# Seven-product gate groups: the fifth sum borrows an accumulator tile, and one of the four summed weight blocks is made by an adding transfer from DRAM

## The chip, the cores and the metric

The kernel runs on one core of one Trainium2 chip. The metric is the device time of that core in microseconds (us), the median of several runs. The core has a matrix engine (TensorE, "PE" in the profile), a vector engine ("DVE"), a scalar engine ("ACT"), a general engine ("POOL") and a queue engine ("SP") that here only issues transfers. Each engine works through its own instructions strictly in program order; what one engine needs of another it waits for with semaphores.

## The reference

Two layers, each on 256 tokens of width 2048. One wide input projection feeds three token mixers and, per mixer b, a sigmoid gate of width 2048:

```python
h = rms_norm(x, norm_w)
proj = h @ w_in
(qa, ka, va, za, qi, ki, wi, ub, zb, qc, kc, vc, zc, gates) = jnp.split(proj, split_points(), axis=-1)
...
y_a = (dsa_attention(...) * jax.nn.silu(za)) @ w_a_out
y_b = (conformer_conv(...) * jax.nn.silu(zb)) @ w_b_out
y_c = (stick_breaking_attention(...) * jax.nn.silu(zc)) @ w_c_out
g = jax.nn.sigmoid(gates).reshape(b, s, N_BRANCH, D_MODEL)
merged = g[:, :, 0] * y_a + g[:, :, 1] * y_b + g[:, :, 2] * y_c
return x + merged @ w_out
```

What matters here are the gates, `h @ w_in[:, gate columns]`, and the products that run between them: the last of `za` and `zb`, and `y_b`, `y_c`, `y_a`.

## The kernel before

**A plain product.** Weights stay in DRAM in float32. A unit is two blocks of 128 rows by 512 columns (512 KB): SP loads it into one of six `raw` tiles, ACT rounds it to the matrix engine's float32r format (`wh`, line 279), and DVE takes what the rounding lost (`wl`, line 284); three tiles of each exist. The activations have been split the same way, so one unit makes three passes (high by high, low by high, high by low) for each of two token blocks: 12 matmuls of 512 columns, all at line 295. `chunk_steps` sums a 512-column chunk over 16 units (or 8, for the branch products) in an accumulator tile `acc` of two PSUM banks; two such tiles exist, in turn, so that one can be read out while the next is filled. After each unit `chunk_steps` yields.

**A seven-product group.** Three of the twelve 512-column pairs of gate chunks in a layer (the list `FAST`) are made by Strassen's scheme in Winograd's form, in the generator `strassen`: two token blocks by two column blocks, the input dimension halved, so that seven block products stand for eight. One product of one unit is 6 matmuls. Each of the four units u of a half is worked off in turn. In the first loop, per u: o1 with block b11, o5 with s5 = b11 + b12, o6 with s6 = s5 + b22, o7 with s7 = b12 + b22. The sums are DVE instructions (`summands`, line 1195). The partial results live in two `mm` tiles of two banks each, one bank per sum. Then the outputs c11, c21 and c22 are formed (lines 1238 to 1242), and the second loop adds, per u: o1 with b21, o7 with s4 = s6 + b21 (again a DVE sum at line 1195, into the place of s6, kept since the first loop), and o5 with b22, which is loaded a second time.

**How both are woven together.** `combine` runs the plain work of this stage: second half of `za`, then `zb` (two chunks), a gate chunk, the four chunks of `y_b`, a gate chunk, the four chunks of `y_c`, the four of `y_a`. After each of its units, a budget `owed` grows by `RATES[kind]`; as long as it is not negative, `advance_fast` takes one step of the group, and the step's own yield (1, 2 or 3) is taken off. A scheduler then puts each engine's instructions in order, those marked high priority first; casts (`high`), differences (`low`), sums and the read-outs of accumulators are so marked. Read-outs differ: `za` and `zb` are read by ACT as two 16-bit copies (`turn_in`, line 172), gate chunks by two Tanh on ACT (line 962), and branch chunks by one DVE instruction that also applies the gate (lines 1157 and 1159).

**The POOL queue.** Gates and parked activations are fetched and stored through `paced`: ACT copies three columns of the newest `wh` (line 245), POOL copies those (line 246), and POOL then issues the transfer, so that it starts no earlier than that point of the weight stream.

Of the kernel before, what the change touches and what calls it, by code (L numbers as in the profile page):

```python
# [15 lines left out]
P = 128  # L16
# [15 lines left out]
TAKEN = -3e38  # L32
RATES = (1.85, 1.85, 1.8, 1.9)
TURN = (8, 8)
# [19 lines left out]
def trunk(ctx: ExitStack, tc: tile.TileContext, x, xt, w_in, w_a, w_b, w_c, w_out,  # L54
# [6 lines left out]
    dp = ctx.enter_context(tc.tile_pool(name="scratch", bufs=1, space=bass.MemoryType.DRAM))  # L61
    ap = ctx.enter_context(tc.tile_pool(name="acc", bufs=2, space=bass.MemoryType.PSUM))
    mp = ctx.enter_context(tc.tile_pool(name="mm", bufs=2, space=bass.MemoryType.PSUM))
# [58 lines left out]
    def mm_tile():  # L122
        return mp.tile([P, 1024], F32, tag="mm", name=nm("mm"))

    def acc_tile():
        return ap.tile([P, 2, 512], F32, tag="acc", name=nm("acc"))

# [113 lines left out]

    def paced(dst, src):
        mark, copy = small(3, 12), small(5, 4)
        with tc.high_priority():
            nc.scalar.copy(mark, landed[0][:, 0, 0:3])  # L245
        seen = nc.gpsimd.tensor_copy(copy[:, :3], mark)  # L246
        with tc.issue_after(seen.ins):
            nc.gpsimd.dma_start(dst, src)

# [106 lines left out]
    def chunk_steps(w, segs, act, nk, ku=2, whole=False):  # L356
        acc = acc_tile()
        n = sum(c for _, c in segs)
        accs = [acc[:, t, :] for t in range(NT)]
        for k0 in range(0, nk, ku):  # L360
            background(token_products(accs, n, unit(w, k0, ku, segs), act, k0, ku, nk, range(NT)))
            yield
        return acc if whole else accs
# [158 lines left out]
    for layer in range(DEPTH):  # L522
# [681 lines left out]
        def strassen(b, jj):  # L1204
            c0 = O_G + b * D + jj * 1024
            kept = []
            pa, pb = mm_tile(), mm_tile()
            o1, o5, o6, o7 = pa[:, :512], pa[:, 512:], pb[:, :512], pb[:, 512:]
            def block(k0, c, u):
# [8 lines left out]
            for u in range(4):  # L1218
# [6 lines left out]
                summands(s5, b22, dst=s6)  # L1225
                kept.append(s6)
                yield 2
                product(o6, mixed(1), u, halves(s6))
                s7 = summands(b12, b22)
                yield 2  # L1230
                product(o7, mixed(3), u, halves(s7))
                if u < 3:
# [4 lines left out]
            with tc.high_priority():  # L1237
                nc.scalar.copy(c11, o1)
                nc.vector.tensor_add(c21, o6, c11)
                nc.vector.tensor_add(c22, o7, c21)  # L1240
                nc.vector.tensor_sub(c22, o5, c22)
                nc.scalar.activation(c22, c22, AF.Tanh, scale=0.5)
            yield 3
            for u in range(4):
                b21 = block(KC, 0, u)
                product(o1, plain(0, KC), u, halves(b21), True)
                s4 = summands(kept[u], b21, dst=kept[u])
                yield 1
                product(o7, plain(1, KC), u, halves(s4), True)
                yield 2  # L1250
                product(o5, mixed(2), u, halves(block(KC, 512, u)), True)
                yield 1
            with tc.high_priority():
                nc.scalar.activation(c11, o1, AF.Tanh, scale=0.5)
                nc.vector.tensor_sub(c12, o5, c21)
                nc.vector.tensor_add(c21, o7, c21)
                nc.scalar.activation(c12, c12, AF.Tanh, scale=0.5)
                nc.scalar.activation(c21, c21, AF.Tanh, scale=0.5)
# [18 lines left out]
        owed = 0  # L1277
        for _ in combine():
            owed += RATES[kind[0]]
            for _ in range(2):  # L1280
                if back:
                    back.pop(0)()
            while owed >= 0 and fast_:
                owed -= advance_fast()

# [126 lines left out]
```

## Time and profile before

Median 2006.66 us of 3 runs (2006.46 to 2009.44). The profiled execution took 2007.48 us, and its span, from the first to the last instruction, is 2005.6 us.

| | busy, us | share of the span | instructions |
|---|---|---|---|
| PE (matmuls) | 1993.7 | 99% | 9518 |
| DVE | 1614.1 | 80% | 1758 |
| ACT | 1402.9 | 70% | 1988 |
| POOL | 119.5 | 6% | 176 |
| read from / written to HBM | 419.59 MB / 23.07 MB | | |
| profiled execution | 2007.48 us | span 2005.6 us | mean granted clock 0.998 |

Both layers pass through the same stages; the woven stage lies at about 560 to 895 us in the first layer and 1555 to 1890 us in the second. Its mean DMA rate is 282 and 285 GB/s there. A row of grouped instructions reads: line, engine, operation, output and input, count, then busy us and mean ns of one. A window row gives busy us and the number of instructions (x) of PE, PE's weight load, DVE, ACT and POOL in that stretch, then the granted clock, the DMA share and GB/s.

### The profile page before, as it was taken

How to read it: one execution, taken by the hardware profiler on the slowest of the kernel's cores; microseconds unless marked ns; L12 is line 12 of the kernel's file. 1: busy time of each engine (PE TensorE's matmuls, PEld its weight loads, DVE VectorE, ACT ScalarE, POOL GpSimd, SP SyncE). 2: the span in 40 equal slices, each digit the busy share in tenths (PEclk: the TensorE clock that was granted, in tenths of full speed). 3: DMA queues.
4: the chain of work that ended last, by engine and by line, in shares of the span. 5: the costliest groups of instructions: out<-in, count | busy, mean ns of one | idle time of the engine just before them, and what ended most of it. 6: DMA issues, size and time to landing. Idle time of an engine off the chain costs nothing.

```text
span 2005.6 us, 26820 instructions
## 1 busy us (share of the span) xinstructions
PE 1993.7 (99%) x9518; PEld 1686.6 (84%) x9518; DVE 1614.1 (80%) x1758; ACT 1402.9 (70%) x1988; POOL 119.5 (6%) x176
## 2 busy tenths in 40 slices
PE   9999999999999999999999999999999999999998
PEld 7888889988888888878888888899888888888887
DVE  8687787897998887886676887778979988878865
ACT  7699877667786755566666997776677776555653
POOL 0000000000000203300000000000000002133000
PEclk9999999999999999999999999999999999999999
DMA  8788667768789879998967776576688999799973
GB/s 281 211 228 214 170 177 211 220 179 219 211 260 288 267 255 302 301 288 250 264 199 213 217 214 177 159 223 207 189 212 219 281 276 281 250 305 316 289 247 126
DMA packets 350902, 471.17 MB, mean 235 GB/s; under 512 B 109488, under 2 KB 167600, under 8 KB 350640
## 3 DMA queue, kind: packets, MB, share of 16 engines
q1 hardware_dynamic: 329216, 425.01, 72.3%
q0 software_dynamic: 20096, 41.95, 7.1%
q10 hardware_dynamic: 1456, 2.51, 0.4%
q8 instruction: 74, 1.21, 0.2%
q14 instruction: 60, 0.49, 0.1%
HBM read 419.59 MB, written 23.07 MB: 221 GB/s over the span
## 4 chain that ended last, share of the span: by engine, by line
PE 96%; DMA 1%; DVE 1%; ACT 1%; issue 0%; ACTq 0%; SPq 0%; DVEq 0%
PE acc L295 82%; PE mm L295 11%; DMA raw<-in_w_in_dram 1%; DVE wl L284 1%; PE mm L940 1%; PE mm L970 1%; ACT wh L279 0%; PE mm L1010 0%; PE mm L805 0%; PE mm L761 0%; PE mm L914 0%; PE mm L789 0%; PE mm L807 0%; DMA cst<-in_consts_dram 0%; PE mm L764 0%
## 5 line engine op out<-in xcount | busy, mean ns | idle before, releaser
L295 PE MATMUL acc<-wh,s 128*128 128x512 f32 (+2 forms) x4480 | 1092.3, 386 | 1.5 <-ACT wh L279 1.5
L284 DVE TENSOR_TENSOR wl<-raw,wh 128x1024 fp32r<-128x1024 f32 (+2 forms) x706 | 848.2, 1208 | 280.0 <-ACT wh L279 258.8
L279 ACT CAST wh<-raw 128x1024 fp32r<-128x1024 f32 (+2 forms) x705 | 730.4, 1040 | 389.1 <-PE acc L295 263.5
L295 PEld LDWEIGHTS acc<-wh,s 128*128 128x128 f32 x4480 | 828.2, 188 | 167.8 <-ACT wh L279 2.4
L295 PE MATMUL acc<-wl,s 128*128 128x512 f32 (+2 forms) x2240 | 589.4, 385 | 0.0
L295 PEld LDWEIGHTS acc<-wl,s 128*128 128x128 f32 x2240 | 415.4, 188 | 84.2 <-DVE wl L284 0.4
L474 ACT ACTIVATE t<-s,cst 128x255 f32<-128x255 f32 (+14 forms) x480 | 201.1, 487 | 0.1
L295 PE MATMUL mm<-wh,s 128*128 128x512 f32 x672 | 180.2, 390 | 0.4 <-ACT wh L279 0.2
L295 PEld LDWEIGHTS mm<-wh,s 128*128 128x128 f32 x672 | 125.7, 188 | 28.0 <-ACT wh L279 1.7
L477 DVE TENSOR_TENSOR s<-s,t 128x1020 f32<-128x1020 f32 (+14 forms) x120 | 138.7, 1156 | 3.4 <-ACT t L474 2.7
L295 PE MATMUL acc<-s,wh 128*128 128x384 f32 (+1 forms) x608 | 126.4, 348 | 0.0
L295 PEld LDWEIGHTS acc<-s,wh 128*128 128x128 f32 x608 | 104.2, 189 | 3.1
L295 PE MATMUL mm<-wl,s 128*128 128x512 f32 x336 | 104.1, 391 | 0.2
L279 ACT CAST wh<-s 128x1024 fp32r<-128x1024 f32 x48 | 50.4, 1049 | 54.6 <-DVE s L1195 31.7
L295 PEld LDWEIGHTS acc<-s,wl 128*128 128x128 f32 x608 | 79.2, 191 | 1.0
L295 PE MATMUL acc<-s,wl 128*128 128x192 f32 (+1 forms) x608 | 79.7, 273 | 0.0
L284 DVE TENSOR_TENSOR wl<-s,wh 128x1024 fp32r<-128x1024 f32 x48 | 58.8, 1225 | 22.0 <-ACT wh L279 21.7
L295 PEld LDWEIGHTS mm<-wl,s 128*128 128x128 f32 x336 | 62.7, 188 | 15.0 <-DVE wl L284 2.3
L963 POOL DMA_DIRECT2D gates<-t x12 | 8.9, 739 | 1113.1 <-ACT t L962 1112.5
L279 ACT CAST wh<-t 128x1024 fp32r<-128x1024 f32 x48 | 50.4, 1050 | 32.4 <-PE acc L295 19.0
L246 POOL COPY sm<-sm 128x3 f32<-128x3 f32 x68 | 53.8, 801 | 310.9 <-ACT sm L245 310.9
L284 DVE TENSOR_TENSOR wl<-t,wh 128x1024 fp32r<-128x1024 f32 x48 | 58.7, 1224 | 13.9 <-ACT wh L279 10.4
(248 smaller groups left out, 1294.7 us busy)
## 6 DMA issues: line engine op xcount, KB each, us to landing
raw<-in_w_in_dram SPq DMA_DIRECT2D x578, 512.0 KB, 4.5
raw<-in_w_out_dram SPq DMA_DIRECT2D x64, 512.0 KB, 5.0
raw<-in_w_b_dram SPq DMA_DIRECT2D x32, 512.0 KB, 5.8
raw<-in_w_c_dram SPq DMA_DIRECT2D x32, 512.0 KB, 5.9
raw<-in_w_a_dram SPq DMA_DIRECT2D x32, 512.0 KB, 6.3
t<-gates POOLq DMA_DIRECT2D x20, 512.0 KB, 7.2
s<-parked POOLq DMA_DIRECT2D x32, 256.0 KB, 7.4
gates<-t POOLq DMA_DIRECT2D x12, 512.0 KB, 6.6
```

Of the source, the lines that this page charges most:

```text
L246: seen = nc.gpsimd.tensor_copy(copy[:, :3], mark)
L279: highs[0] = nc.scalar.copy(u[1], u[0])
L284: sub = nc.vector.tensor_sub(u[2], u[0], u[1].bitcast(F32))
L295: newest[0] = nc.tensor.matmul(o, lhsT, rhs, start=start, stop=stop, skip_group_check=True)
L474: nc.scalar.activation(o[:, i, :S - d], yT[:, c, :S - d], AF.Copy, scale=wq)
L477: sums.append(lambda: nc.vector.tensor_add(to, to, o[:, :, :S - d]))
L940: nc.tensor.matmul(ps[:, q * S:(q + 1) * S], qb2[i][:, g * 4 + q, :], ki[:, j, 0, :], start=n == 0, stop=n == 2)
L963: nc.gpsimd.dma_start(gates[b][:, :, j * 512:(j + 1) * 512].rearrange("t p d -> p t d"), sg_)
L970: nc.tensor.matmul(ps[:, q * n:(q + 1) * n], qaT[:, c * 4 + q, ts_], kaT[:, c, :n], start=True, stop=True)
```

## The change

Five sums now run in the first loop: the product o3 with b22 moves there, so that b22 is used while it is still in its `raw` tile, and the second loop has two products instead of three. The fifth sum needs a PSUM bank, and both `mm` tiles are full; `lend` takes the accumulator tile that the running chunk does not use. The two accumulator tiles get names of their own (`acc`, `acd`), and while one is lent, every chunk uses the other one. The loan ends after the first loop, when o3 has been read. At the end of a chunk inside the loan (`chunk_steps` now yields True there) at least two steps of the group are put between it and the next. The sum s4 is made by an adding transfer: b21 is sent from DRAM by POOL onto s6 (`paced(..., accum_op=ALU.add)`), once o6's operands have been made from s6. `RATES` goes down, since a group has fewer steps of larger yield. The four outputs are formed with the same five DVE instructions in another order. The number of matmuls does not change.

```diff
-RATES = (1.85, 1.85, 1.8, 1.9)
+RATES = (1.7, 1.7, 1.7, 1.75)
...
+    turn_of = [0]
+    lent = [None]
     def acc_tile():
-        return ap.tile([P, 2, 512], F32, tag="acc", name=nm("acc"))
+        turn_of[0] = 1 - turn_of[0] if lent[0] is None else 1 - lent[0]
+        return ap.tile([P, 2, 512], F32, tag=("acc", "acd")[turn_of[0]], name=nm("acc"))
+
+    def lend():
+        lent[0] = 1 - turn_of[0]
+        return ap.tile([P, 2, 512], F32, tag=("acc", "acd")[lent[0]], name=nm("acc"))[:, 0, :]
...
-            yield
+            yield k0 + ku == nk
...
-            o1, o5, o6, o7 = pa[:, :512], pa[:, 512:], pb[:, :512], pb[:, 512:]
+            o1, o7, o5, o6 = pa[:, :512], pa[:, 512:], pb[:, :512], pb[:, 512:]
+            o3 = lend()
...
                 summands(s5, b22, dst=s6)
-                kept.append(s6)
                 yield 2
                 product(o6, mixed(1), u, halves(s6))
                 s7 = summands(b12, b22)
                 yield 2
+                product(o3, mixed(2), u, halves(b22))
+                kept.append(s6)
+                paced(s6, place(KC, 0, u), accum_op=ALU.add)
+                yield 1
                 product(o7, mixed(3), u, halves(s7))
...
-                nc.vector.tensor_add(c22, o7, c21)
-                nc.vector.tensor_sub(c22, o5, c22)
+                nc.vector.tensor_sub(c12, o5, c21)
+                nc.vector.tensor_sub(c22, c12, o7)
+                nc.vector.tensor_add(c12, o3, c12)
...
+            lent[0] = None
...
             for u in range(4):
-                b21 = block(KC, 0, u)
-                product(o1, plain(0, KC), u, halves(b21), True)
-                s4 = summands(kept[u], b21, dst=kept[u])
+                product(o1, plain(0, KC), u, halves(block(KC, 0, u)), True)
                 yield 1
-                product(o7, plain(1, KC), u, halves(s4), True)
-                yield 2
-                product(o5, mixed(2), u, halves(block(KC, 512, u)), True)
+                product(o7, plain(1, KC), u, halves(kept[u]), True)
                 yield 1
...
-        for _ in combine():
+        for ends in combine():
...
-            while owed >= 0 and fast_:
-                owed -= advance_fast()
+            if True:
+                least = 2 if ends and lent[0] is not None else 0
+                while (owed >= 0 or least > 0) and fast_:
+                    least -= 1
+                    owed -= advance_fast()
```

Three places show how the order moves. They are told for the first layer; the second has the same order. In changed rows the line numbers are shifted: 295 became 303, 279 became 287, 284 became 292, 172 became 180, 188 became 196.

**PE, where zb's first chunk ends.** Before, the chunk's accumulator is `acc_5417` and the next chunk's is `acc_5674`, in the other tile:

```order
L295 MATMUL mm_5162<-wl_5643,s_775_4565 128x512 x2
L295 MATMUL acc_5417<-wh_5653,s_11_102 128x512 x8
L295 MATMUL acc_5417<-wl_5654,s_11_102 128x512 x4
L295 MATMUL acc_5674<-wh_5676,s_8_99 128x512 x8
L295 MATMUL acc_5674<-wl_5677,s_8_99 128x512 x4
```

Now the chunk's accumulator is `acc_5432`, the next one's `acc_5710` in the same tile, and `acc_5163` is o3 in the lent tile:

```order
L303 MATMUL acc_5432<-wh_5663,s_11_102 128x512 x8
L303 MATMUL acc_5432<-wl_5664,s_11_102 128x512 x4
L303 MATMUL mm_5162<-wh_5680,s_772_4562 128x512 x4
L303 MATMUL mm_5162<-wl_5681,s_772_4562 128x512 x2
L303 MATMUL mm_5162<-wh_5694,s_773_4563 128x512 x4
L303 MATMUL mm_5162<-wl_5695,s_773_4563 128x512 x2
L303 MATMUL acc_5163<-wh_5751,s_774_4564 128x512 x4
L303 MATMUL acc_5710<-wh_5712,s_8_99 128x512 x8
```

Where the next chunk followed at once, 16 matmuls of the group now stand between.

**ACT, at the same place.** Before, the two copies that read `acc_5417` out:

```order
L279 CAST wh_5653<-raw_5652 128x1024
L279 CAST wh_5676<-raw_5675 128x1024
L279 CAST wh_5701<-raw_5700 128x1024
L188 COPY t_940_5413<-t_941_5414 128x1024
L279 CAST wh_5723<-raw_5721 128x1024
L172 COPY t_992_5670<-acc_5417 128x2x512
L1238 COPY t_998_5693<-mm_5161 128x512
L172 COPY t_992_5670<-acc_5417 128x2x512
```

And now those that read `acc_5432` (`raw_5690` is b22, and `wh_5751` is o3's operand):

```order
L287 CAST wh_5680<-t_987_5632 128x1024
L287 CAST wh_5694<-s_999_5692 128x1024
L287 CAST wh_5712<-raw_5711 128x1024
L196 COPY t_944_5428<-t_945_5429 128x1024
L287 CAST wh_5733<-raw_5732 128x1024
L180 COPY t_1003_5706<-acc_5432 128x2x512
L287 CAST wh_5751<-raw_5690 128x1024
L180 COPY t_1003_5706<-acc_5432 128x2x512
```

The cast for o3, whose matmuls stand ahead of the next chunk on PE, stands on ACT behind the casts of the next chunk's first two units, behind a copy of an older chunk and behind the first read-out copy; the second read-out copy is last.

**DVE, in the second loop of the third group, during y_a.** Before (`s_1346_7251` is a kept s6, which becomes s4):

```order
L284 TENSOR_TENSOR wl_7763<-raw_7760,wh_7762 128x1024
L1195 TENSOR_TENSOR s_1346_7251<-s_1346_7251,raw_7760 128x1024
L284 TENSOR_TENSOR wl_7774<-s_1346_7251,wh_7773 128x1024
L1159 SCALAR_TENSOR_TENSOR t_1441_7646<-t_1441_7646,acc_7652 128x1024
L284 TENSOR_TENSOR wl_7799<-raw_7797,wh_7798 128x1024
```

Now (`s_1361_7285` is a kept s6 onto which the transfer has added b21):

```order
L1171 TENSOR_TENSOR s_878_5135<-s_878_5135,t_1464_7708 128x1024
L292 TENSOR_TENSOR wl_7862<-raw_7860,wh_7861 128x1024
L292 TENSOR_TENSOR wl_7883<-raw_7880,wh_7882 128x1024
L292 TENSOR_TENSOR wl_7894<-raw_7892,wh_7893 128x1024
L292 TENSOR_TENSOR wl_7911<-s_1361_7285,wh_7910 128x1024
L292 TENSOR_TENSOR wl_7923<-raw_7920,wh_7922 128x1024
```

The sum between the two differences of one u is gone.

More of the change, by code (lines that the diff above doesn't have):

```diff
@@ L61, in trunk @@
     dp = ctx.enter_context(tc.tile_pool(name="scratch", bufs=1, space=bass.MemoryType.DRAM))
-    ap = ctx.enter_context(tc.tile_pool(name="acc", bufs=2, space=bass.MemoryType.PSUM))
+    ap = ctx.enter_context(tc.tile_pool(name="acc", bufs=1, space=bass.MemoryType.PSUM))
     mp = ctx.enter_context(tc.tile_pool(name="mm", bufs=2, space=bass.MemoryType.PSUM))
@@ L240, in trunk, with paced @@
     highs = [None]
-    def paced(dst, src):
+    def paced(dst, src, **kw):
         mark, copy = small(3, 12), small(5, 4)
@@ L247, in paced @@
         with tc.issue_after(seen.ins):
-            nc.gpsimd.dma_start(dst, src)
+            nc.gpsimd.dma_start(dst, src, **kw)
     def operands(shape):
@@ L1207, in strassen, with place @@
             pa, pb = mm_tile(), mm_tile()
-            o1, o5, o6, o7 = pa[:, :512], pa[:, 512:], pb[:, :512], pb[:, 512:]
+            o1, o7, o5, o6 = pa[:, :512], pa[:, 512:], pb[:, :512], pb[:, 512:]
+            o3 = lend()
+            def place(k0, c, u):
+                return w[(k0 + 2 * u) * P:(k0 + 2 * u + 2) * P, c0 + c:c0 + c + 512].rearrange("(k p) c -> p k c", p=P)
             def block(k0, c, u):
@@ L1239, in strassen @@
                 nc.vector.tensor_add(c21, o6, c11)
-                nc.vector.tensor_add(c22, o7, c21)
-                nc.vector.tensor_sub(c22, o5, c22)
+                nc.vector.tensor_sub(c12, o5, c21)
+                nc.vector.tensor_sub(c22, c12, o7)
+                nc.vector.tensor_add(c12, o3, c12)
                 nc.scalar.activation(c22, c22, AF.Tanh, scale=0.5)
+                nc.scalar.activation(c12, c12, AF.Tanh, scale=0.5)
+            lent[0] = None
             yield 3
             for u in range(4):
-                b21 = block(KC, 0, u)
-                product(o1, plain(0, KC), u, halves(b21), True)
-                s4 = summands(kept[u], b21, dst=kept[u])
+                product(o1, plain(0, KC), u, halves(block(KC, 0, u)), True)
                 yield 1
-                product(o7, plain(1, KC), u, halves(s4), True)
-                yield 2
-                product(o5, mixed(2), u, halves(block(KC, 512, u)), True)
+                product(o7, plain(1, KC), u, halves(kept[u]), True)
                 yield 1
@@ L1254, in strassen @@
                 nc.scalar.activation(c11, o1, AF.Tanh, scale=0.5)
-                nc.vector.tensor_sub(c12, o5, c21)
                 nc.vector.tensor_add(c21, o7, c21)
-                nc.scalar.activation(c12, c12, AF.Tanh, scale=0.5)
                 nc.scalar.activation(c21, c21, AF.Tanh, scale=0.5)
```

## Prediction

> **What bounds the kernel now.** I read the page's first part, then who PE waited for, then windows of 50 us, to see whether PE has anything to give.
>
> ```profile
> span 2005.6 us, 26820 instructions
> PE 1993.7 (99%) x9518; PEld 1686.6 (84%) x9518; DVE 1614.1 (80%) x1758; ACT 1402.9 (70%) x1988; POOL 119.5 (6%) x176
> ...
> PE 96%; DMA 1%; DVE 1%; ACT 1%; issue 0%; ACTq 0%; SPq 0%; DVEq 0%
> ```
> ```profile
> PE acc L295 <- ACT wh L279: 1.5, 2, 1.1
> PE mm L657 <- DVE eps L75: 1.1, 1, 1.1
> PE mm L562 <- DVE t L682: 0.3, 1, 0.3
> PE mm L295 <- ACT wh L279: 0.2, 1, 0.2
> ```
>
> PE is the chain (96%), and its visible waits are about 3 us in 2005.6. The number of matmuls stays, so time can only come from moments in which PE runs thinner than it could. Since ends of matmuls are modelled, I count starts instead of waits:
>
> ```profile
> 800.00:850.00 50.00, 50.00 (x222) 41.42 (x221) 43.03 (x38) 27.91 (x37) 16.14 (x25) 1.00 0.99 302
> 850.00:900.00 50.00, 49.59 (x214) 39.35 (x213) 41.93 (x39) 31.61 (x34) 2.41 (x4) 1.00 0.95 291
> ...
> 1800.00:1850.00 50.00, 50.00 (x222) 41.40 (x221) 43.85 (x39) 27.70 (x37) 15.57 (x26) 1.00 1.00 305
> 1850.00:1900.00 50.00, 49.82 (x218) 40.30 (x217) 42.05 (x39) 32.94 (x35) 1.55 (x3) 1.00 0.96 295
> ```
>
> A full window holds 222 starts, 50 / 222 = 0.225 us each. The windows that end the woven stage hold 214 and 218: 8 and 4 are missing, 1.8 and 0.9 us. **All that the woven stages lose is 2.7 us**, at a granted clock of 1.00; every other window between 560 and 850 us holds 222 or 223. What ends last in the gaps stands in the chain:
>
> ```profile
> 849.93 14.59 DMA raw<-in_w_in_dram
> ...
> 866.85 1.23 DVE s L1195
> ...
> 868.17 1.06 ACT wh L279
> ...
> 869.26 1.24 DVE wl L284
> ...
> 870.54 0.73 PE mm L295 x2
> ```
>
> From 866.85 on it is the second loop's sum s4: sum, cast, difference, then matmul, 3.7 us in series (around 880 and in the second layer at 1871 it is the same).
>
> **The change part by part.** My base is the profiled execution, 2007.48 us (span 2005.6 and 1.9 around it); the median shown, 2006.66, lies 0.82 lower, and I carry the sum over to it.
>
> *s4 goes from DVE.* Two layers with three groups of four units make 24 sums:
>
> ```profile
> L1195 DVE TENSOR_TENSOR s<-s,raw 128x1024 f32<-128x1024 f32 x24 | 29.3, 1219 | 0.0
> ```
>
> 29.3 us of DVE work go, but DVE is not the bound; only the serial path in the gaps is worth something. Without s4, the second loop's two products per unit need 2 differences of 1.22 us for 12 matmuls (2.7 us), and the cast of a kept block can start as soon as a `wh` tile is free. What is late next there is the landing of b21. I take the full **-2.7 us**; its ends are 0 (DMA was the cause after all) and -2.7.
>
> *The loads.* 24 second loads of b22 disappear from SP, but b21 now crosses twice, once as operand and once in the adding transfer: 24 x 512 KB move from the SP queue to POOL's, and HBM read stays at 419.59 MB. So nothing is gained where DMA binds. What an adding transfer from DRAM costs is not in the trace; the nearest rows are the one from SBUF and a plain fetch on the same queue:
>
> ```profile
> raw<-in_w_in_dram SPq DMA_DIRECT2D x578, 512.0 KB, 4.5
> ...
> t<-gates POOLq DMA_DIRECT2D x20, 512.0 KB, 7.2
> ...
> s<-t POOLq DMA_DIRECT2D x8, 512.0 KB, 7.8
> ```
>
> The result is needed only in the second loop, tens of us later, so its 7.8 us are hidden; adding may cost the shared DMA engines 7.8 - 7.2 = 0.6 us. If each one held the weight stream up by that, 24 x 0.6 = 14.4 us; but PE feels late loads only where it already ran thin, in the third group, so 8 x 0.6 = **4.8 us is my upper end**. The lower end is 0, since fewer SP loads cannot give PE more than the 2.7 us above. I take **0**, by the row nearest to a price on PE:
>
> ```profile
> ACT wh L279 <- DMA raw<-in_w_in_dram: 26.4, 14, 3.7
> ```
>
> ACT already waits 26.4 us for weights, and PE loses at most those 2.7.
>
> *Marks.* Each adding transfer brings a mark on ACT and a copy on POOL:
>
> ```profile
> L246 POOL COPY sm<-sm 128x3 f32<-128x3 f32 x68 | 53.8, 801 | 310.9 <-ACT sm L245 310.9
> ...
> L245 ACT COPY sm<-wh 128x3 f32<-128x3 f32 x68 | 10.1, 191 | 2.5
> ```
>
> 24 x 0.19 = 4.6 us on an ACT that is 70% busy, and 24 x 0.8 on an idle POOL. Behind them in POOL's queue stand only gate and parked transfers, needed a chunk later: nothing.
>
> *One accumulator for the chunks.* This is a new wait: a chunk's first matmul waits until the chunk before it has been read out, and everything behind it on PE waits too. Until now a whole chunk hid that. The cover now is the group steps between, and I go through the boundaries with these rows:
>
> ```profile
> L284 DVE TENSOR_TENSOR wl<-raw,wh 128x1024 fp32r<-128x1024 f32 x686 | 834.0, 1222 | 262.0 <-ACT wh L279 245.1 <-ACT t L771 10.0 <-ACT t L1242 3.8
> ...
> L1159 DVE SCALAR_TENSOR_TENSOR t<-t,acc 128x1024 f32<-128x1024 f32 x16 | 19.5, 1218 | 4.8 <-PE acc L295 4.7
> ```
> ```profile
> L962 ACT ACTIVATE t<-acc 128x512 f32<-128x512 f32 x24 | 13.4, 591 | 0.0
> ```
> ```profile
> 589.11 1.04 ACT L279 CAST wh<-raw 128x1024 fp32r<-128x1024 f32 x1
> 590.06 1.00 ACT L172 COPY t<-acc 128x1024 uint16<-128x1024 uint16 x1
> 590.96 1.05 ACT L279 CAST wh<-t 128x1024 fp32r<-128x1024 f32 x1
> 591.91 1.01 ACT L172 COPY t<-acc 128x1024 uint16<-128x1024 uint16 x1
> 593.15 1.06 ACT L279 CAST wh<-raw 128x1024 fp32r<-128x1024 f32 x1 [0.24 <-PE acc L295]
> ...
> 621.77 1.36 ACT L188 COPY t<-t 128x1024 uint16<-128x1024 uint16 x1
> 623.08 1.06 ACT L279 CAST wh<-raw 128x1024 fp32r<-128x1024 f32 x1
> ```
> ```profile
> 591.14 1.98 PE L295 MATMUL acc<-wh,s 128*128 128x512 f32 x8
> 592.96 1.07 PE L295 MATMUL acc<-wl,s 128*128 128x512 f32 x4
> 593.86 1.07 PE L295 MATMUL mm<-wh,s 128*128 128x512 f32 x4
> 594.77 0.62 PE L295 MATMUL mm<-wl,s 128*128 128x512 f32 x2
> 595.22 1.07 PE L295 MATMUL mm<-wh,s 128*128 128x512 f32 x4
> ```
>
> A unit of a chunk takes 593.86 - 591.14 = 2.72 us, a group product 1.36. Back to back, a cast on ACT takes 0.95 us and a read-out copy 0.90, an older copy (L188) 623.08 - 621.77 = 1.31; the cast at 593.15 begins 0.19 us after 592.96, where PE left the `wh` tile that it fills (three tiles, reused in turn). Let T be the moment when PE passes a chunk's last matmul.
>
> The seven boundaries per layer that DVE reads out, behind y_b's and y_c's chunks: two products cover 2.72 us; in the order, the read-out stands behind the differences for just those two products and at most one sum. By the reuse of the `wl` tiles these are done by about T + 0.5, so it ends by T + 0.5 + 1.22 = T + 1.7: 1.0 us to spare, no wait. The two behind gate chunks are read by two Tanh of 0.59 us from T + 0.24, done by T + 1.4; the covers are 2.72 and 1.36: nothing. za's end: first copy at T + 0.24, a cast, second copy from T + 2.1, done at T + 3.1; the cover is 14 matmuls, 3.17: just nothing.
>
> zb's first end is the one that doesn't fit. ACT's order there: the cast of the next chunk's first unit, once its tile is free at T - 0.91 + 0.19 = T - 0.72; the older copy from T + 0.23; the second cast T + 1.54; the first read-out copy T + 2.49; the cast for o3 T + 3.39, done at T + 4.4. PE has 12 matmuls until then and wants o3 at T + 2.72: **it waits 1.7 us**, and with the 0.1 us that PE loses on restarting (the pair at 870.54, after a stall, takes 0.73 where 0.62 is normal, as at 594.77) 1.8. Then 4 matmuls, until T + 5.35, meet the second copy's end at T + 5.3. Both layers have this order: 2 x 1.8 = **+3.7 us**, unrounded. The ends: 0, if ACT runs further ahead, and 2 x (2.7 + 1.8), if the older copy also waits for its transposes.
>
> Sum: -2.7 + 0 + 3.7 = +1.0. From 2007.48 that is 2008.5; carried to the median, **2007.7 us**.
>
> **A rule against the change.** The boundary rows above say that reading out hides behind the group's products. The Trainium skill, Perfetto Trace Analysis, section Matmuls, advises rotating independent matmul groups through different PSUM banks so that the reading-out of one overlaps the next group's matmuls. By that rule every boundary now shows a wait. The trace agrees that rotation works (no PE wait at any boundary before), but has no run without it; the second rival below prices that.
>
> **The rivals.**
> 1. *No boundary waits.* ACT has slack, and PE's order might find o3's cast early. Against it: casts can't pass the copies in ACT's order. Then 2006.66 - 2.7 = 2004.0, within 0.2%.
> 2. *The cover is too short at DVE's boundaries: slower.* Today DVE reads out late, without harm:
>
> ```profile
> 852.38 1.98 PE L295 MATMUL acc<-wh,s 128*128 128x512 f32 x8
> ...
> 854.34 1.21 DVE L1159 SCALAR_TENSOR_TENSOR t<-t,acc 128x1024 f32<-128x1024 f32 x1
> ```
> The read-out started 1.96 us after its chunk was passed at 852.38. With 1.22 for itself it would end at 3.18, 0.46 beyond a cover of 2.72. It decides from a start later than T + 1.5. For it: that row. Against: three output sums stood ahead there, and at the new boundaries none does. 14 x 0.46 = 6.4 on top of my sum: 2014.1.
> 3. *The gaps at the end stay*, since loads and not s4 make them: the load at 849.93 took 14.59 us in the chain, where 4.5 is the median. Then 2007.7 + 2.7 = 2010.4, still within 0.2%.
> 4. *Adding transfers crowd the weight stream* in the third group, where the DMA share is already 0.99 and 1.00: 2007.7 + 4.8 = 2012.5, slower.
> 5. *Faster by over 0.2%* (4.0 us) would need more than the 2.7 us that PE loses: no row offers it.
>
> **How the numbers follow.** About 0.2% is what a measurement of this kernel can tell from no change: 2002.6 to 2010.7. Chances: forecast 0.45, rival 1 0.20, rival 3 0.12, rival 2 0.10, rival 4 0.08, rival 5 0.05. Same: 0.45 + 0.20 + 0.12 = 0.77; slower 0.18; faster 0.05. The range runs from rival 1 to rival 4, 2003.8 to 2012.5, and leaves out rivals 2 and 5.
>
> **What would show it.** Right: windows that end the woven stage hold 222 again; no instruction at line 1203 (once 1195) that writes a kept `s`; near 625 and 1620 us a PE wait of about 1.7 us on ACT, for o3's `wh`; SP's queue down to about 412 MB, POOL's up to 54. Wrong: PE waits on DVE's read-out at chunk ends, new waits on DMA in the third group, or gaps left at 850 to 900.

## The result, and the profile after

The changed kernel takes **2024.11 us** (median of 4 runs, 2023.72 to 2025.23), the kernel before beside it 2008.05 us (4 runs, 2006.46 to 2009.94): a ratio of 1.0081, 95% interval 1.0063 to 1.0098. It is slower by 16 us, and outside the predicted range. Its profiled execution took 2023.76 us with a span of 2022.0.

The prediction's own list of signs comes first. These are the queues and the memory traffic on the page of after (packets, MB, share):

```profile
q1 hardware_dynamic: 322688, 412.43, 70.4%
q0 software_dynamic: 26624, 54.53, 10.2%
HBM read 419.59 MB, written 23.07 MB: 219 GB/s over the span
```

SP's queue is down to 412 MB and POOL's up to 54, with the same read: the transfers moved as foretold. Next, what PE waited for in after (us in total, times, longest):

```profile
PE mm L303 <- DVE t L1257: 8.3, 2, 4.2
PE acc L303 <- ACT wh L287: 4.2, 3, 1.9
```

Two of the three waits in the second row, 1.95 and 1.94 us, are the foretold wait on ACT. The first was not foretold: twice, PE waits for the vector sum at line 1257, one of the four that form a group's outputs. The windows of PE alone (busy us, starts of matmuls, granted clock, DMA share, GB/s) say what each place costs:

```profile
600.00:650.00 50.00, 48.05 (x205) 0.97 1.02 269
...
850.00:900.00 50.00, 45.77 (x195) 0.97 0.96 286
1600.00:1650.00 50.00, 48.06 (x213) 1.00 1.04 291
...
1850.00:1900.00 50.00, 45.97 (x191) 0.93 0.97 291
```

With those from 740 to 790 and from 1740 to 1790 us, which are full (222 each), these windows start 1248 matmuls; before they started 1320 (first row of the table below). The 72 that are missing, at 0.225 us each, are 16.2 us, and the span grew by 16.4: nearly the whole loss lies in four places (a further wait of 0.8 us, near 1510 us, lies outside the woven stage). The end of zb's first chunk (near 625 and 1629 us) lost 17 + 9 = 26 starts, 5.9 us. The third group's turn from its first to its second loop (near 871 and 1873 us) lost 19 + 27 = 46 against before, 10.4 us, although the 8 + 4 that were missing there before should have come back. Against a full window it lost 27 + 31 = 58, 13 us.

The timeline of after at that turn (start us, us, engine, line, operation, what ended the idle time before):

```profile
868.26 0.58 ACT L1254 COPY t<-mm 128x512 f32<-128x512 f32 x1
...
869.54 0.68 DVE L1255 TENSOR_TENSOR t<-mm,t 128x512 f32<-128x512 f32 x1
...
870.26 0.69 DVE L1256 TENSOR_TENSOR t<-mm,t 128x512 f32<-128x512 f32 x1
870.31 1.07 PE L303 MATMUL acc<-wl,s 128*128 128x512 f32 x4
872.56 1.05 ACT L287 CAST wh<-raw 128x1024 fp32r<-128x1024 f32 x1 [3.71 <-DMA raw<-in_w_in_dram]
...
873.63 1.23 DVE L292 TENSOR_TENSOR wl<-raw,wh 128x1024 fp32r<-128x1024 f32 x1 [2.69 <-ACT wh L287]
874.78 0.68 DVE L1257 TENSOR_TENSOR t<-t,mm 128x512 f32<-128x512 f32 x1
...
875.60 0.94 PE L303 MATMUL mm<-wh,s 128*128 128x512 f32 x3 [4.23 <-DVE t L1257]
```

Read it from below. PE's next product goes into o1, whose tile now also holds o7, and L1257 is the sum that reads o7. L1257 could have run at 870.95, behind L1256, but DVE's order has the difference of b21 between them, and that waits for the cast of a block that landed late (ACT idle 3.71 us on a DMA). The order of the two kernels at this place, before (its lines 1240 and 1241 are the sums, `wl_7692` is b21's difference) and after (`wl_7841`):

```
L1240 TENSOR_TENSOR t_1440_7638<-mm_7050,t_1439_7637 128x512
L1241 TENSOR_TENSOR t_1440_7638<-mm_7049,t_1440_7638 128x512
L1159 SCALAR_TENSOR_TENSOR t_1398_7482<-t_1398_7482,acc_7488 128x1024
L284 TENSOR_TENSOR wl_7692<-raw_7689,wh_7691 128x1024
```
```
L1255 TENSOR_TENSOR t_1479_7779<-mm_7078,t_1479_7779 128x512
L1256 TENSOR_TENSOR t_1480_7780<-mm_7078,t_1479_7779 128x512
L292 TENSOR_TENSOR wl_7841<-raw_7838,wh_7840 128x1024
L1257 TENSOR_TENSOR t_1480_7780<-t_1480_7780,mm_7077 128x512
L1258 TENSOR_TENSOR t_1480_7780<-acc_7079,t_1480_7780 128x512
```

Before, every sum stood ahead of the block's difference; now two stand behind it. There are also more of them: of the five DVE instructions that form a group's outputs, three stood at the turn before and four do now, so it is not quite "the same five DVE instructions in another order".

The loads were not this late before either. The kernel before, DMA issues from 840 to 880 us (count, KB each, median us from issue to landing):

```profile
raw<-in_w_a_dram SPq DMA_DIRECT2D x9, 512.0 KB, 7.5
raw<-in_w_in_dram SPq DMA_DIRECT2D x7, 512.0 KB, 9.3
```

In after the medians of these two rows are 12.3 and 14.3 us. The turn also lies elsewhere: its last sum began at 853.73 us before and at 875.49 after.

### The profile page after: what moved, and what is told of

It is laid out like the page before. It is cut to its first block, busy times and chain, and to the rows that moved or that the text cites. A ratio compares the mean times of both kernels' runs of the same rounds, so it can differ in the third digit from the quotient of the medians.

```text
span 2022.0 us, 26932 instructions
## 1 busy us (share of the span) xinstructions
PE 1998.7 (99%) x9518; PEld 1691.1 (84%) x9518; DVE 1589.7 (79%) x1734; ACT 1406.2 (70%) x2012; POOL 165.0 (8%) x224
## 4 chain that ended last, share of the span: by engine, by line
PE 64%; issue 31%; DMA 2%; ACT 1%; DVE 1%; POOL 0%; ACTq 0%; SPq 0%; DVEq 0%; POOLq 0%
PE acc L303 53%; PE mm L303 9%; DMA raw<-in_w_in_dram 1%; ACT wh L287 1%; DMA t<-t 0%; DVE wl L292 0%; DMA raw<-in_w_c_dram 0%; PE mm L1018 0%; DMA gates<-t 0%; PE mm L948 0%; PE mm L978 0%; ACT t L999 0%; DMA cst<-in_consts_dram 0%; PE mm L813 0%; PE mm L769 0%
## 5 line engine op out<-in xcount | busy, mean ns | idle before, releaser
L303 PE MATMUL acc<-wh,s 128*128 128x512 f32 (+2 forms) x4576 | 1122.9, 387 | 4.2 <-ACT wh L287 4.2
L303 PEld LDWEIGHTS acc<-wh,s 128*128 128x128 f32 x4576 | 849.0, 189 | 176.8 <-ACT wh L287 5.4
L303 PE MATMUL acc<-wl,s 128*128 128x512 f32 (+2 forms) x2288 | 604.1, 385 | 0.8 <-DVE wl L292 0.8
L303 PEld LDWEIGHTS acc<-wl,s 128*128 128x128 f32 x2288 | 425.3, 188 | 87.1 <-DVE wl L292 1.3
L303 PE MATMUL mm<-wh,s 128*128 128x512 f32 x576 | 155.5, 391 | 8.3 <-DVE t L1257 8.3
L303 PEld LDWEIGHTS mm<-wh,s 128*128 128x128 f32 x576 | 108.3, 188 | 31.5 <-issue 9.0
L254 POOL COPY sm<-sm 128x3 f32<-128x3 f32 x92 | 75.0, 819 | 358.6 <-ACT sm L253 358.5
L303 PE MATMUL mm<-wl,s 128*128 128x512 f32 x288 | 88.6, 389 | 0.0
L303 PEld LDWEIGHTS mm<-wl,s 128*128 128x128 f32 x288 | 54.1, 188 | 11.2
```

The source lines that it names most:

```text
L303: newest[0] = nc.tensor.matmul(o, lhsT, rhs, start=start, stop=stop, skip_group_check=True)
```

## The experiments

Every run is the changed kernel with one edit, or with edits joined. The table has the starts of matmuls in the same six windows of each profiled run, so that a place can be compared (222 is full; one execution each, and a place shifts by some us between runs), the median and the ratio to the kernel before.

| run | 600 to 650 | 740 to 790 | 850 to 900 | 1600 to 1650 | 1740 to 1790 | 1850 to 1900 | span, us | median, us | ratio, 95% interval |
|---|---|---|---|---|---|---|---|---|---|
| before | 222 | 222 | 214 | 222 | 222 | 218 | 2005.6 | 2008.05 | |
| after | 205 | 222 | 195 | 213 | 222 | 191 | 2022.0 | 2024.11 | 1.0081, 1.0063 to 1.0098 |
| e1 pairing | 204 | 222 | 193 | 203 | 223 | 193 | 2023.9 | 2025.58 | 1.0088, 1.0071 to 1.0105 |
| e3 sum on DVE | 212 | 201 | 190 | 213 | 200 | 189 | 2031.5 | 2034.35 | 1.0137, 1.0120 to 1.0154 |
| e4 more cover | 221 | 193 | 188 | 219 | 192 | 190 | 2039.2 | 2041.36 | 1.0168, 1.0153 to 1.0183 |
| e5 earlier | 216 | 192 | 223 | 219 | 193 | 223 | 2020.5 | 2023.38 | 1.0077, 1.0062 to 1.0092 |
| e6 sums ahead | 205 | 222 | 204 | 205 | 222 | 216 | 2015.9 | 2013.97 | 1.0028, 1.0017 to 1.0040 |
| e7 load early | 206 | 222 | 181 | 205 | 222 | 186 | 2027.6 | 2028.51 | 1.0099, 1.0084 to 1.0114 |
| e8 cover za, zb | 221 | 222 | 197 | 221 | 222 | 189 | 2020.9 | 2022.71 | 1.0074, 1.0059 to 1.0089 |
| e9: e6 + e7 + e8 | 221 | 222 | 185 | 221 | 222 | 187 | 2024.8 | 2026.33 | 1.0093, 1.0078 to 1.0108 |
| e10: e6 without adding | 212 | 223 | 210 | 212 | 221 | 218 | 2011.7 | 2015.21 | 1.0036, 1.0024 to 1.0048 |
| e11: e6 + e8 | 222 | 223 | 215 | 221 | 221 | 216 | 2012.2 | 2013.10 | 1.0027, 1.0016 to 1.0038 |
| e12: e6 + e5 | 216 | 199 | 222 | 220 | 195 | 222 | 2017.2 | 2018.89 | 1.0058, 1.0041 to 1.0075 |
| e13: e6 + burst sooner | 212 | 223 | 214 | 213 | 222 | 221 | 2010.2 | 2012.82 | 1.0027, 1.0016 to 1.0037 |
| e14: e6 + copy on DVE | 218 | 222 | 217 | 218 | 222 | 214 | 2013.6 | 2015.39 | 1.0036, 1.0022 to 1.0049 |
| e15: e6 + e13 + e14 | 218 | 222 | 212 | 217 | 222 | 221 | 2010.1 | 2013.79 | 1.0031, 1.0019 to 1.0043 |

### e1: the tiles paired as before

```diff
-            o1, o7, o5, o6 = pa[:, :512], pa[:, 512:], pb[:, :512], pb[:, 512:]
+            o1, o5, o6, o7 = pa[:, :512], pa[:, 512:], pb[:, :512], pb[:, 512:]
```

> Only the assignment of the four sums to the two tiles goes back to that of the kernel before (o1 and o5 in one tile, o6 and o7 in the other). Theory T (shared tile): at the start of the third group's second loop PE's first product writes o1 in a tile that also holds o7, and waits for the vector sum that reads o7, which stands behind the difference of the late block. Without that sharing PE starts when the block's cast is done: of the gaps of 4.62 and 4.42 us about 2.6 us each stay, so 2 x 1.9 us plus some of the half-clock matmuls behind them go: 2019 to 2021 us. Rival L (late load): the block's landing sets the start whatever the tiles; gaps unchanged within 0.5 us, 2023 to 2025 us.

2025.58 us: the expectation of the shared tile fell. The row of PE's waits and the timeline at the turn say why:

```profile
PE acc L303 <- DVE t L1258: 8.0, 2, 4.0
```
```profile
870.90 0.69 DVE L1257 TENSOR_TENSOR t<-t,mm 128x512 f32<-128x512 f32 x1
...
874.23 1.22 DVE L292 TENSOR_TENSOR wl<-raw,wh 128x1024 fp32r<-128x1024 f32 x1 [2.64 <-ACT wh L287]
...
875.38 0.68 DVE L1258 TENSOR_TENSOR t<-acc,t 128x512 f32<-128x512 f32 x1
...
876.21 3.33 PE L303 MATMUL acc<-wh,s 128*128 128x512 f32 x7 [3.94 <-DVE t L1258]
```

L1257 now runs ahead of the difference, but L1258, which reads o3, still stands behind it, and PE's next chunk needs the borrowed accumulator back. A wait of the same length stays while any sum that frees a tile stands behind the late block. With this edit the scheduler also moved three matmuls of b21's product on PE from ahead of the next chunk's unit to behind it, so PE now meets the accumulator first, and what the shared tile costs alone is not tested.

### e3: the fourth sum on VectorE again

```diff
-                paced(s6, place(KC, 0, u), accum_op=ALU.add)
...
-                product(o1, plain(0, KC), u, halves(block(KC, 0, u)), True)
+                b21 = block(KC, 0, u)
+                product(o1, plain(0, KC), u, halves(b21), True)
+                s4 = summands(kept[u], b21, dst=kept[u])
                 yield 1
-                product(o7, plain(1, KC), u, halves(kept[u]), True)
+                product(o7, plain(1, KC), u, halves(s4), True)
```

> The adding transfer from DRAM goes; the fourth sum is made by VectorE from the loaded block in the second loop, as before, and everything else of the changed kernel stays, the borrowed accumulator too. Theory A (adding transfers make the block late): the block lands in 7 to 8 us instead of 12 to 14, the gaps of 4.62 and 4.42 us shrink below 1 us with the half-clock matmuls behind them (-13 us), while the serial path of the sum comes back (+2.7 us): 2013 to 2015 us. Rival L (parked words, gate words and weights alone crowd the DMA engines): gaps stay above 3 us, and 2.7 us come on top: 2025 to 2028 us. The wait at the boundary near 625 us is the same by both.

2034.35 us, slower than either theory said, and with a third long wait in each layer (201 and 200 starts at 740 to 790). Again PE waits for an output sum (L1256 is L1257 of after):

```profile
PE mm L303 <- DVE t L1256: 12.5, 4, 3.2
```

So the adding transfers alone are not what makes the wait. As a test of the loads it is blurred, since the order of the sums differs too; e10 repeats it with that order fixed.

### e4 and e5: the place of the boundaries moved

e4 sets `least = 4` for `least = 2`; e5 sets `RATES` back to (1.85, 1.85, 1.8, 1.9).

> Four instead of two steps of the seven-product group are put behind each accumulator boundary while a tile is lent, so PE has 12 or 18 narrow matmuls in place of 6 or 12 before it needs the accumulator again. Theory Z (ScalarE's order of copies at the boundary near 625 us): the gaps of 2.34 and 2.33 us there go, with the eight half-clock matmuls behind the first, 4 to 6 us less, if the third group's start is as before: 2018 to 2020 us. Rival (the gap is only moved to the next boundary or to the loads, because the group's products come in lumps): within 2 us of 2024.

> Only the pace numbers go back to those of the kernel before (1.85, 1.85, 1.8, 1.9), so the seven-product groups are woven in sooner and the third group's second loop starts about one chunk (15 us) earlier, ahead of the eight parked transfers. Theory L (the block is late because of that burst): the gaps of 4.62 and 4.42 us go with their half-clock matmuls, 2011 to 2015 us. Theory T (tile shared by o1 and o7 with the sum behind the block's difference): the wait shrinks to what VectorE needs, about 2 us each, 2017 to 2021 us. If neither holds: 2024 and more, since the faster pace meets the loads earlier elsewhere.

e4: 2041.36 us, the worst of all. zb's windows are full again (221, 219), but the 740 and 850 windows lose 29 to 34 starts each. e5: 2023.38, no gain by theory L or T: the third group's turn is clean (223 starts), and the wait has gone to the second group's turn (192). So e4 adds a wait at the second group's turn, and e5 moves the wait there: it belongs to the end of a first loop, not to the third group.

### e6: the four sums ahead of the block's difference

```diff
-                nc.vector.tensor_add(c12, o3, c12)
+                summed = nc.vector.tensor_add(c12, o3, c12)
...
-                product(o1, plain(0, KC), u, halves(block(KC, 0, u)), True)
+                b21 = (block(KC, 0, u), *operands([P, 2, 512]))
+                high(b21)
+                with tc.issue_after(summed.ins):
+                    low(b21)
+                product(o1, plain(0, KC), u, b21[1:], True)
```

> Two theories fell: tiles paired as before left the gaps (then PE waited for the last of the four sums, which frees the borrowed tile), and without the adding transfer they stayed too. In every run with a long gap PE waits for one of the vector sums at the end of a group's first loop, and that sum stands in VectorE's order behind the difference of the second loop's first block. Here only that order changes: the difference is issued behind all four sums. Theory Q (VectorE's order passes the block's lateness on): the sums end near 873, PE starts with the block's cast, and the gaps of 4.62 and 4.42 us fall to about 2.6 us each: 2018 to 2021 us. Rival L (the block itself is what PE waits for): gaps above 4 us, 2023 to 2025 us.

2013.97 us: **10 of the 16 us are back** with nothing but the order of instructions. DVE's order is what was edited, but the scheduler moved others with it: three matmuls of b21's product on PE now stand behind the next chunk's unit, and on ACT a Tanh stands ahead of a cast. PE's order is not the cause: by the trace's tile names it is that of e1 from end to end, and there PE still waited 8.0 us. The turn in e6, and PE's wait there:

```profile
870.59 1.23 DVE L292 TENSOR_TENSOR wl<-raw,wh 128x1024 fp32r<-128x1024 f32 x1 [2.78 <-ACT wh L287]
871.74 0.68 DVE L1255 TENSOR_TENSOR t<-mm,t 128x512 f32<-128x512 f32 x1
...
873.90 0.69 DVE L1258 TENSOR_TENSOR t<-acc,t 128x512 f32<-128x512 f32 x1
...
874.47 1.05 ACT L287 CAST wh<-raw 128x1024 fp32r<-128x1024 f32 x1 [3.43 <-DMA raw<-in_w_in_dram]
```
```profile
PE acc L303 <- DVE t L1258: 3.4, 2, 2.1
```

The block is as late as before (ACT waits 3.43 us for it), but the sums no longer are: they end at 874.6, before that cast is done. PE's waits at the two turns fall from 8.3 to 3.4 us. PE's wait for L1258 in the first layer is 2.14 us, until 874.74. Theory Q holds. In the profiled executions the two turns have 34 starts more than in after (204 and 216 against 195 and 191), 7.7 us. That execution was e6's slowest, 2017.82 us; the median lies below the 2018 to 2021 of the theory, probably since fewer slow matmuls follow in most executions (see the last section): the mean granted clock is 0.998 in the median run and 0.994 to 0.995 in the runs of after. What is left at the turn comes from the load of a plain chunk, whose cast waited 2.67 us for it and whose difference (870.59) still stands ahead of the sums, and at zb nothing has changed.

### e7 and e9: the first block loaded earlier

```diff
                 if u < 3:
                     b11, b12, s5 = firsts(u + 1)
+                else:
+                    b21 = block(KC, 0, 0)
...
-                product(o1, plain(0, KC), u, halves(block(KC, 0, u)), True)
+                product(o1, plain(0, KC), u, halves(block(KC, 0, u) if u else b21), True)
```

e9 joins this with the edits of e6 and e8.

> Only the load of the second loop's first block is issued earlier, where the first loop's last step would have loaded the next step's blocks; VectorE's order of sums and difference stays. Theory L (the load's lateness starts the chain; with the block there, its difference does not hold up the sums): the gaps of 4.62 and 4.42 us fall below 1 us, with the half-clock matmuls behind them: 2010 to 2013 us. Theory Q alone (the order matters even with the block in time, since difference and sums then still take 4 us on VectorE in series): gaps of 1 to 2.5 us, 2014 to 2019 us. If the earlier load only pushes the other loads back: unchanged or slower.

> The three edits together: the sums ahead of the difference, the block loaded earlier, four steps behind a boundary in the two gate stages. By theories Q, L and Z together nothing long is left: the gaps go, and what remains is the change's own gain of some 2.7 us: 2004 to 2008 us, no slower than the kernel before. If lumps of products make new waits: 2012 us or more.

2028.51 and 2026.33 us: theory L as put (load it earlier, and the wait goes) fell; the time is what e7's last case, an earlier load that only pushes the others back, had said. In e7 (whose L1256 is L1254 of after) the weight of the chunk beside it is late instead, and the copy with which the sums begin stands behind that cast on ACT:

```profile
873.06 1.04 ACT L287 CAST wh<-raw 128x1024 fp32r<-128x1024 f32 x1 [3.50 <-DMA raw<-in_w_a_dram]
874.01 0.58 ACT L1256 COPY t<-mm 128x512 f32<-128x512 f32 x1
```

In e9 it is the same, with 3.90 us of waiting for that weight, although its sums stand ahead of the difference: PE waits 6.29 us. One of six `raw` tiles taken earlier is one less for the chunk's stream, so the likely reading is that the lateness is shared by the loads of that time, and moving one ahead of another only changes which is late.

### e8 and e11: more cover in za and zb alone

```diff
-                least = 2 if ends and lent[0] is not None else 0
+                least = (4 if kind[0] == 2 else 2) if ends and lent[0] is not None else 0
```

> Four steps of the group instead of two behind a boundary, but only in the two gate stages, where ScalarE reads the accumulator out. Theory Z (the wait near 625 us is ScalarE's order of casts and copies, with too few matmuls over it): the gaps of 2.34 and 2.33 us shrink below 1 us and the half-clock matmuls behind the first go; the third group's gaps stay: 2018 to 2020 us. Rival (as with four steps everywhere, the lump of products brings the group's end forward, and its sums meet a late load elsewhere): a new gap of 4 to 6 us in each layer in the 700s or 1700s, 2026 us or more.

> e6 and e8 together: the sums ahead of the difference, and four steps behind a boundary in the two gate stages. If the two causes add, the gaps of 2.33 us near 626 and 1627 us with their half-clock matmuls (3.5 us each) go and small ones of 0.5, 0.8 and 0.4 us come in each layer, as in e8, 3 to 4 us less than e6's 2014: 2009 to 2011 us. If the moved products meet the late load again, as in e9: 2016 us or more.

e8: zb's windows are full (221, 221), the time is 2022.71; e11: 2013.10, which cannot be told from e6. The wait at zb can be covered, but smaller waits come elsewhere (in e8 0.3 to 0.7 us each, near 595, 701 and 710 us and again in the second layer) and take part of it back: both times lie 2 to 3 us above their expectations.

### e10 and e13: why the blocks are late

e10 is e6 with e3's edit. e13 is e6 with the eight parked transfers released one chunk sooner; PE and DVE keep e6's order:

```diff
-                    if n == 1 and j == 3:
+                    if n == 1 and j == 2:
                         ahead = unpark(0)
```

> As e6 (the sums of the first loop ahead of the first block's difference), but without the adding transfers: the fourth sum is made on VectorE in the second loop, as in e3. What stays in e6 at the third group's start is 2.53 and 1.67 us. Theory A (adding transfers make the block late): these gaps fall below 1 us; the sum's serial path costs some 2.5 us in each layer, as the small gaps of 1.0 and 1.4 us in e3 show: 2013 to 2016 us. Theory B (the parked words, gate words and weights of that moment are enough to make it late): gaps of 1.5 us or more stay there and 2 x 2.5 us come on top: 2017 to 2020 us.

> e6 with the parked transfers released one chunk earlier (about 16 us). Theory B (they make the blocks late): of e6's gaps of 2.53 and 1.67 us at the third group's end less than 0.5 us is left, with the half-clock matmuls behind the first, and the weight blocks of that time land in 8 to 10 us instead of 13 to 14: 2008 to 2011 us. Rival (the DMA engines are full there whatever is moved, as at 0.97 of the time in the kernel before): gaps within 0.7 us of e6's, 2013 to 2016 us.

The DMA issues from 840 to 880 us (count, KB each, median us to landing), in e6, then e10, then e13:

```profile
raw<-in_w_a_dram SPq DMA_DIRECT2D x8, 512.0 KB, 13.2
s<-parked POOLq DMA_DIRECT2D x8, 256.0 KB, 9.3
raw<-in_w_in_dram SPq DMA_DIRECT2D x4, 512.0 KB, 14.0
```
```profile
raw<-in_w_a_dram SPq DMA_DIRECT2D x9, 512.0 KB, 12.0
...
raw<-in_w_in_dram SPq DMA_DIRECT2D x4, 512.0 KB, 11.2
```
```profile
raw<-in_w_a_dram SPq DMA_DIRECT2D x10, 512.0 KB, 10.5
raw<-in_w_in_dram SPq DMA_DIRECT2D x4, 512.0 KB, 10.2
...
s<-parked POOLq DMA_DIRECT2D x4, 256.0 KB, 7.8
```

Without adding transfers (and with 24 loads of 512 KB fewer) the blocks land 1 to 3 us sooner, but PE still waits 2.47 us at the first layer's turn (210 starts), and the time, 2015.21, is not below e6's. The expected cost of the sum on DVE (2.5 us a layer) did not appear either: the time is what theory A said, the gap what theory B said. With the parked transfers partly moved (four of eight remain in that stretch), no wait on an output sum is left and the second layer's window is full (221); in the first layer a smaller wait, 1.12 us, came instead until 854.9 us. The median, 2012.82, lies 1 us below e6's, inside its interval: what the parked transfers do is shown by the rows, not by the time. Neither edit alone brings back the 7.5 and 9.3 us of the kernel before.

### e12: the turn with loads in time

> e6 and e5 together: the sums ahead of the difference, and the pace numbers of the kernel before, so that the third group's second loop starts ahead of the parked transfers. Theory Q: e5's gaps of 4.75 us at the second group's end fall by 2 us or more each with the half-clock matmuls behind them, and nothing stays at the third group: 2012 to 2015 us. If the place of the second group's end has a late block of its own that PE needs, the gaps stay above 3.5 us: 2018 us or more.

2018.89 us: the time of the second case, but not for its reason. At the second group's turn in e12 no cast waits for a DMA, and PE waits all the same:

```profile
744.40 0.61 PE L303 MATMUL mm<-wl,s 128*128 128x512 f32 x2
744.65 1.05 ACT L287 CAST wh<-raw 128x1024 fp32r<-128x1024 f32 x1 [0.80 <-PE mm L303]
...
745.60 0.58 ACT L1254 COPY t<-mm 128x512 f32<-128x512 f32 x1
746.21 0.69 DVE L1255 TENSOR_TENSOR t<-mm,t 128x512 f32<-128x512 f32 x1 [0.15 <-ACT t L1254]
...
747.73 0.69 DVE L1257 TENSOR_TENSOR t<-t,mm 128x512 f32<-128x512 f32 x1
...
748.57 1.16 PE L303 MATMUL mm<-wh,s 128*128 128x512 f32 x4 [3.55 <-DVE t L1257]
```

Here o7's last product is followed by o1's next one with nothing between. So the serial path of a cast, the copy and three sums is itself the price of the turn: 3.55 us from 745.0, when PE ends, even with every load in time.

### e14 and e15: the older copy off ScalarE

```diff
-            done.append(turn_in(a, None, partial(gated, k), slots[k // 4], turn))
+            done.append(turn_in(a, None, partial(gated, k), slots[k // 4], turn, early=turn == LATE))
```

> e6 with one copy of each gate chunk (the second word copy after the transposes, 1.35 us on ScalarE) on VectorE. Theory Z (the prediction's step: the older copy stands between the casts on ScalarE): the gap of 2.33 us at the first end of the second gate stage falls to 1.0 to 1.3 us and no half-clock matmuls follow: 2 to 5 us less than e6's 2014, 2009 to 2012 us. Rival (the chain from accumulator to copy and cast is long enough without it, or VectorE becomes late in its place): the gap stays above 1.8 us, 2013 to 2016 us.

> e6, e13 and e14 together. If Z and B both hold, no gap over 1.3 us is left: 2005 to 2009 us, within 0.2% of the kernel before. If B falls: as e14. Nothing in these theories makes it faster than the kernel before by more than the 2.7 us of small gaps that the change took away.

The first end of zb in after, then in e14 (ACT's instructions and PE's next ones):

```profile
622.11 1.05 ACT L287 CAST wh<-raw 128x1024 fp32r<-128x1024 f32 x1
623.06 1.35 ACT L196 COPY t<-t 128x1024 uint16<-128x1024 uint16 x1
624.28 1.03 ACT L287 CAST wh<-raw 128x1024 fp32r<-128x1024 f32 x1
625.22 1.00 ACT L180 COPY t<-acc 128x1024 uint16<-128x1024 uint16 x1
626.12 1.04 ACT L287 CAST wh<-raw 128x1024 fp32r<-128x1024 f32 x1
627.07 1.01 ACT L180 COPY t<-acc 128x1024 uint16<-128x1024 uint16 x1
...
627.22 4.60 PE L303 MATMUL acc<-wh,s 128*128 128x512 f32 x12 [1.95 <-ACT wh L287]
```
```profile
622.92 1.04 ACT L287 CAST wh<-raw 128x1024 fp32r<-128x1024 f32 x1
623.87 1.00 ACT L180 COPY t<-acc 128x1024 uint16<-128x1024 uint16 x1
624.77 2.00 ACT L287 CAST wh<-raw 128x1024 fp32r<-128x1024 f32 x2
...
626.82 3.03 PE L303 MATMUL acc<-wh,s 128*128 128x512 f32 x12 [0.74 <-ACT wh L287]
```

After's six ACT instructions are the six of the prediction, in its order. With the older copy (L196) gone from among them, PE's wait falls from 1.95 to 0.74 us, by about that copy's length, and no slow matmuls follow: the step is shown. The time, 2015.39, is no better than e6's, because DVE, which now has the copy, is late with differences elsewhere, as PE's waits in e14 show:

```profile
PE acc L303 <- DVE wl L292: 3.4, 3, 1.9
```

e15 joins all and gains nothing over e13. No version beats the kernel before; its missing starts were 12, 2.7 us, so there was little to win.

## Why the prediction was wrong

- **PE as the bound, and 2.7 us to win**: right as far as the runs go. Where the third group's turn is clear of trouble (e5), its windows hold 223 and 223 instead of 214 and 218. The reading that only s4's serial path made the gaps is doubtful: e10 has that sum on DVE and shows no such gaps.
- **Loads, adding transfers and marks at nothing**: the queues moved as said; e6 against e10 (2013.97 and 2015.21) shows no net cost in time of the adding transfers. The loads near the turn did come later than before, though (12.3 and 14.3 us instead of 7.5 and 9.3). Rival 4 (adding transfers crowd the stream) had a true core in the landing times, 1 to 3 us, but without these transfers the turn's wait stays (e3, e10). The marks were not tried alone.
- **A slip in the range**: its lower end, 2003.8, is given as rival 1, whose own time is 2004.0; nothing hangs on it.
- **The seven boundaries read by DVE, gate chunks and za's end, no wait**: right in after, where no row of PE's waits names them. So rival 2 did not come. The Trainium skill's advice to rotate PSUM banks (Perfetto Trace Analysis, Matmuls) is not refuted by that: 2.7 us of other products covered these read-outs, and where the last reader came later, at the turn, the wait was there (at zb PE waited for a cast that stood behind a read-out).
- **zb's first end, 1.7 us of wait**: right in place, mechanism and near in size (1.95); e14 shows the mechanism. The term, 3.7 us for both layers, was too small: it came to 26 starts, 5.9 us, because in the first layer a train of half-speed matmuls follows the gap (17 starts lost there, 9 in the second layer), which the sum had not at all.
- **The step that failed** is that the turn had no term. The prediction took "the same five DVE instructions in another order" for nothing and wrote of the second loop: "What is late next there is the landing of b21", at no cost. But after the change there is a fourth sum at the turn, and the sums free one thing more than before, the borrowed accumulator that the next chunk needs, beside o1's tile, which they had to free before too (it held o5 then and holds o7 now). Two of the four had slipped behind the difference of that very block, and what it waited, PE waited: 8.3 us, with the slow matmuls behind it 13 us against full windows. e6, with the sums ahead, takes back 7.7 us of it in the profiled executions and 10 us in the medians. Rival 3 (gaps at the end stay, since loads make them) named the late load, but priced it with the old gaps. The places that the prediction looked at were the chunks' ends, not the end of the borrowing.
- What made the loads late is in part the parked transfers near them: e13 moves four of the eight away, and no wait is left at the third group's turn. The adding transfers add 1 to 3 us (e10), and e5, with the old `RATES`, has its third turn some 13 us sooner and no wait there. How the lateness divides among the three is open. What remains of e6 over the kernel before, some 6 us, is zb's wait, the rest of the late load and small waits that move with every edit; no single run takes them all away. e11's cover and e13's earlier release together were not run.

## What to carry to other kernels

Where a change makes a read-out release something that the bound engine needs (a bank, a lent buffer), price the whole way from the last producer to the last reader, and look in each in-order queue at what stands ahead of every reader, above all instructions that wait for a transfer. An instruction that can be late through no fault of its own belongs behind those that free a resource. And a wait on PE costs more than its own length if the clock falls after it.

## What had not been expected of the hardware

After a gap of about 2.3 us or more between the starts of two matmuls (1.9 us or more of waiting) PE often ran slowly for a while. Windows of after behind the two waits at zb (PE, weight load, DVE, ACT and POOL, granted clock, DMA share, GB/s):

```profile
627.60:630.80 3.20, 3.20 (x9) 2.44 (x9) 2.25 (x2) 2.57 (x4) 1.63 (x2) 0.51 1.02 325
1631.00:1634.00 3.00, 3.00 (x13) 2.42 (x14) 2.46 (x3) 2.83 (x4) 1.57 (x2) 1.00 0.98 337
```

In the first layer the granted clock falls to 0.51, and 3.2 us hold 9 starts where 14 would be normal; in the second layer, after the same wait, it stays at 1.00. The rows of 12 matmuls above show the same: 4.60 us in after at 627.22, 3.03 in e14 after a wait of 0.74. At this place both layers had it in e6, neither in e10 and e13. Such a train cost 1.6 us there (4.60 less 3.03), some 7 starts, so it probably adds to the spread of the runs (e6: 2012.35 to 2017.82, and its profiled run, with three trains, was the slowest). The Trainium skill, TensorE: Matmul & The Clock Gate, Part 1, gives about 3.4 us of idling as what brings the half clock back; here gaps of 2.3 us between starts did so in some executions, so the measured rows decide: in this kernel less idling can be enough, and it is not enough every time. What decides between the two was not tried.
